# The two halves of each weight made by transfers instead of a cast and a subtraction, with ten buffers for each half

## The chip, the cores and the metric

The kernel runs on one core of a Trainium2 chip. The metric is the device time of one launch in microseconds (us), all inputs lying in device memory at its start. A smaller number is better. The time before is the median of three runs, 2927.23 us (2926.73 to 2929.2).

## The reference

A small transformer backbone: two layers over 512 latent tokens and 256 context tokens of width 1024. Each layer is a half-weighted SwiGLU feed-forward block, a token mixer, and another such block; each is modulated by vectors computed from a conditioning vector, and closed by a layer norm. Cut to what matters here, float32 throughout:

```python
def swiglu(u, w_in, w_out):
    a, v = jnp.split(u @ w_in, 2, axis=-1)
    return (jax.nn.silu(a) * v) @ w_out

def ffn_sublayer(h, shift, scale, gate, w_in, w_out, g, b):
    y = swiglu(modulate(h, shift, scale), w_in, w_out)     # h * (1 + scale) + shift
    return layer_norm(ALPHA * h + FFN_RES * gate * y, g, b)

for i in range(DEPTH):                                      # 2
    h_lat, h_ctx = ffn_sublayer(...), ffn_sublayer(...)     # first block
    y = neighborhood_attention(...) if i == 0 else window_gqa(...)
    h_lat = layer_norm(ALPHA * h_lat + m_lat[5] * y_lat, ...)
    h_lat = ffn_sublayer(...)                               # second block (and h_ctx in layer 0)
return h_lat
```

Mixer 0 is a two-dimensional neighbourhood attention with a learned relative bias; mixer 1 is a windowed attention with rotary positions. All weights together are some 158 blocks of 1 MB.

## The kernel before

**The arithmetic.** TensorE multiplies a rounded kind of float32, here called F32R. To keep float32 accuracy every factor is held as two F32R tiles: the hi part, its rounded value, and the lo part, what is left of it. A product is three matmuls (`mm3`, lines 114 to 116): hi by hi, lo activation by hi weight, hi activation by lo weight. The names are `uh`/`ul` for the modulated input, `gh`/`gl` for the gated middle of a feed-forward block, `wh`/`wl` for the weights, `z` for the residual stream, `pa`, `pv`, `pd`, `pq`, `pk` for tiles of PSUM.

**The weights.** The host lays them out in the order of use as units of 128 x 2048. `wunit` (lines 86 to 103) fetches a unit as four tiles of 128 x 512 float32, 256 KB each. For each tile SP issues a load into a raw tile `wr` (three buffers), ACT copies it with rounding to `wh` (line 99), and POOL subtracts the two into `wl` (line 100). `wh` and `wl` have nine buffers each, handed out in turn, so a tile's copy waits until TensorE has read the tile nine back. The last unit of each feed-forward block takes its tiles from another pool instead (`slabs`), and a few units are fetched a second time (`again`, tiles with a b at the end of their names).

**The stages.** A feed-forward block (`ffn`) runs over 11 chunks of 256 middle columns; each chunk uses three units, two for the up projections and one for the down projection. The tokens are taken in two groups, 512 latent and 256 context tokens; the last block (1b) has only the latent ones, in two groups of 256. So 1b spends fewer matmuls on each unit than the other blocks. The mixers (`na_mixer`, `wa_mixer`) project queries, keys and values with such units; in the softmax POOL scales the rows (line 565, `scale_p`), and in mixer 1 POOL also makes one product of the rotary positions (line 763). At the start, four steps (`gemv`) multiply a modulation weight `wm` (1 MB pieces issued by SP) with the conditioning vectors, and the first matmuls with weights go in between. Two more modulation pieces (`wm` 4 and 5) follow in `late_gate`. `bias_tables` (lines 580 to 584) builds the relative bias of mixer 0 in device memory with 8 transfers into `xd` and 16 into `yd`, all issued by SP. Its first part is tied behind the latest weight load (`behind(..., loaded[0])`, a tie that holds only between instructions of the same engine). In the background DVE computes the other modulation vectors from `wt` tiles that SP loads.

**The order.** A scheduler simulates the program and sets the order of each engine's queue; each engine then runs its queue in that order. A DMA is issued by an engine's queue (SP, ACT or POOL) once what it waits for has come; a wait at the head of a queue holds all that stands behind it.

Of the kernel before, what the change touches and what calls it, by code (L numbers as in the profile page):

```python
# [8 lines left out]
F32 = mybir.dt.float32  # L9
F32R = mybir.dt.float32r  # L10
BF16 = mybir.dt.bfloat16
I32 = mybir.dt.int32
AF = mybir.ActivationFunctionType
ALU = mybir.AluOpType
# [4 lines left out]
P = 128  # L19
# [17 lines left out]
def hybrid_kernel(ctx: ExitStack, tc: tile.TileContext, h0, cc, crow, wmod, wmodt, bmod, lnp, wst,  # L37
                  rpbp, nmask, sinks, ropec, rmat, ident, wmask, out):
    nc = tc.nc
    cp = ctx.enter_context(tc.tile_pool(name="cp", bufs=1))  # L40
    rp = ctx.enter_context(tc.tile_pool(name="rp", bufs=1))
    wp = ctx.enter_context(tc.tile_pool(name="wp", bufs=1))
# [41 lines left out]
    wpos, loaded = [0], [None]  # L84

    def wunit(slabs=False, again=None):
        i = wpos[0] if again is None else again
        if again is None:
            wpos[0] += 1
        hs, ls = [], []  # L90
        for q in range(4):
            nm = f"{i}_{q}" + ("" if again is None else "b")
            raw = wp.tile([P, 512], F32, tag="wr", name=f"wr{nm}", bufs=3)
            loaded[0] = nc.sync.dma_start(raw[:], wst[i, :, q * 512:(q + 1) * 512])
            if slabs:
                hi, lo = [sp.tile([P, 512], F32R, tag="slab", name=f"w{x}{nm}", bufs=SLABS) for x in "hl"]
            else:
                hi, lo = [wp.tile([P, 512], F32R, tag=f"w{x}", name=f"w{x}{nm}", bufs=9) for x in "hl"]
            nc.scalar.copy(hi[:], raw[:])  # L99
            nc.gpsimd.tensor_tensor(out=lo[:], in0=raw[:], in1=hi[:].bitcast(F32), op=ALU.subtract)  # L100
            hs.append(hi)
            ls.append(lo)
        return hs, ls
# [295 lines left out]
    def ffn(nm, groups, gt, mid, post, units=(), opened={}, head=None, apart=None):  # L399
# [4 lines left out]
        def unit(slabs=False):  # L404
            return units.pop(0) if units else wunit(slabs)
# [32 lines left out]
        for ci in list(range(NCH)) + [("r", NCH - 2)]:  # L438
# [3 lines left out]
            if late:  # L442
                again = i0
            w = [wunit(again=again + i) if r else unit(ci == NCH - 1 and i == 2) for i in range(3)]
            cn = f"r{ci[1]}" if r else f"{ci}"
            gs = [[gp.tile([P, NT], F32R, tag="gs", name=f"g{x}{nm}_{cn}_{i}", bufs=6) for x in "hl"] for i in range(2)]
# [13 lines left out]
            if r:  # L460
                avs((b, 0), (b, 1))
                dn(b)
                post(1)
            elif late:
                avs((a, 0), (a, 1))
                dn(a)
            elif ci == NCH - 1:
                avs((a, 0), (a, 1))
                dn(a)
                avs((b, 0), (b, 1))  # L470
                post(0)
                dn(b)
            elif ci == 0 and apart:
                apart()
                avs((head[0], 0), (head[0], 1))
                dn(head[0])
                w[0:2] = [wunit(again=i0 + i) for i in range(2)]
                avs(*[(g, i) for g in head[1:] for i in range(2)])
                for g in head[1:]:
                    dn(g)  # L480
            else:
                avs(*([(g, i) for g in head for i in range(2)] if ci == 0 else [(a, 0), (b, 0), (a, 1), (b, 1)]))
                dn(a)
                dn(b)
# [624 lines left out]
```

## Time and profile before

| | us |
|---|---|
| median of 3 runs | 2927.23 |
| the profiled execution's own time | 2926.03 |
| its span, from the first to the last instruction | 2924.2 |
| TensorE (PE) busy | 2802.8 |
| DVE busy | 1842.5 |
| POOL busy | 1247.8 |
| ACT busy | 1033.0 |
| time of the packets of queue q1, as a share of 16 DMA engines | 32.1% |

The profile is of one execution. PE is the matmul side of TensorE, PEld its weight loads. A group's row names line, engine, operation, output and inputs, count, then busy time and the mean of one in ns, then the idle time of the engine before them with what ended it. A row of waits names who waited, for whom, the total, the number of times and the longest. In a view by time, a row is a start, a duration and the instructions merged in it; a bracket holds the idle time before. "SPq" marks what SP's queue issues.

### The profile page before, as it was taken

How to read it: one execution, taken by the hardware profiler on the slowest of the kernel's cores; microseconds unless marked ns; L12 is line 12 of the kernel's file. 1: busy time of each engine (PE TensorE's matmuls, PEld its weight loads, DVE VectorE, ACT ScalarE, POOL GpSimd, SP SyncE). 2: the span in 40 equal slices, each digit the busy share in tenths (PEclk: the TensorE clock that was granted, in tenths of full speed). 3: DMA queues.
4: the chain of work that ended last, by engine and by line, in shares of the span. 5: the costliest groups of instructions: out<-in, count | busy, mean ns of one | idle time of the engine just before them, and what ended most of it. 6: DMA issues, size and time to landing. Idle time of an engine off the chain costs nothing. (4 is left out here: it accounts for less than half of the span.)

```text
span 2924.2 us, 49325 instructions
## 1 busy us (share of the span) xinstructions
PE 2802.8 (96%) x18106; PEld 2470.4 (84%) x18106; DVE 1842.5 (63%) x5023; ACT 1033.0 (35%) x2122; POOL 1247.8 (43%) x1102
## 2 busy tenths in 40 slices
PE   8899999989999979999999899999998999899997
PEld 5788888888888869888888788888887777799997
DVE  3489994375545685767675757776358667733335
ACT  4122122266455452222223522121236655533333
POOL 4233232465433563332335623232456544644453
PEclk9999999999999989999999999999999999899998
DMA  7444442232211312343432324342321111233332
GB/s 290 147 148 145 134 138 61 85 89 80 66 50 52 108 60 87 109 126 109 122 96 87 112 87 121 108 125 73 87 85 55 51 37 30 76 94 96 97 108 81
DMA packets 165842, 286.05 MB, mean 98 GB/s; under 512 B 25952, under 2 KB 38368, under 8 KB 164576
## 3 DMA queue, kind: packets, MB, share of 16 engines
q1 hardware_dynamic: 165312, 282.76, 32.1%
q8 instruction: 142, 2.33, 0.3%
q14 instruction: 100, 0.82, 0.1%
q10 hardware_dynamic: 288, 0.14, 0.0%
HBM read 280.74 MB, written 6.48 MB: 98 GB/s over the span
## 5 line engine op out<-in xcount | busy, mean ns | idle before, releaser
L100 POOL TENSOR_TENSOR wl<-wr,wh 128x512 fp32r<-128x512 f32 x632 | 834.4, 1333 | 1226.7 <-ACT wh L99 1002.3
L99 ACT CAST wh<-wr 128x512 fp32r<-128x512 f32 x632 | 388.9, 620 | 738.4 <-DMA wr<-in_wst_dram 324.4
L172 DVE CUSTOM_DVE_ANT_0 jk<-wt,cb 128x256 f32<-128x256 f32 x960 | 489.3, 544 | 0.0
L395 DVE SCALAR_TENSOR_TENSOR z<-pd1a,gt,z 128x512 f32<-128x512 f32 (+1 forms) x168 | 103.0, 619 | 89.8 <-PE pd1a L116 89.6
L395 DVE SCALAR_TENSOR_TENSOR z<-pd0a,gt,z 128x512 f32<-128x512 f32 (+1 forms) x168 | 102.9, 618 | 83.9 <-PE pd0a L116 83.4
L395 DVE SCALAR_TENSOR_TENSOR z<-pd0b,gt,z 128x256 f32<-128x256 f32 (+1 forms) x176 | 105.0, 600 | 76.6 <-PE pd0b L116 76.5
L114 PE MATMUL pa0a<-uh,wh 128*128 128x512 f32 (+1 forms) x328 | 113.8, 347 | 14.8 <-ACT wh L99 10.9
L114 PE MATMUL pd0a<-gh0a,wh 128*128 128x512 f32 (+1 forms) x336 | 114.9, 345 | 2.9 <-DVE z L395 2.9
L114 PE MATMUL pd0b<-gh0b,wh 128*128 128x256 f32 (+1 forms) x352 | 116.7, 334 | 0.3 <-DVE z L395 0.3
L115 PE MATMUL pd0b<-gl0b,wh 128*128 128x256 f32 (+1 forms) x352 | 116.7, 332 | 0.0
L116 PE MATMUL pd0b<-gh0b,wl 128*128 128x256 f32 (+1 forms) x352 | 116.6, 332 | 0.0
L114 PE MATMUL pa1a<-uh,wh 128*128 128x512 f32 (+1 forms) x336 | 114.7, 341 | 1.2 <-DVE uh L259 1.2
L114 PE MATMUL pd1a<-gh1a,wh 128*128 128x512 f32 (+1 forms) x336 | 113.7, 342 | 1.3 <-DVE z L395 0.7
L114 PE MATMUL pv1a<-uh,wh 128*128 128x512 f32 (+1 forms) x336 | 114.6, 341 | 0.0
L115 PE MATMUL pv1a<-ul,wh 128*128 128x512 f32 (+1 forms) x336 | 114.5, 341 | 0.0
L115 PE MATMUL pa1a<-ul,wh 128*128 128x512 f32 (+1 forms) x336 | 114.3, 340 | 0.0
L116 PE MATMUL pd0a<-gh0a,wl 128*128 128x512 f32 (+1 forms) x336 | 114.3, 341 | 0.0
L115 PE MATMUL pd0a<-gl0a,wh 128*128 128x512 f32 (+1 forms) x336 | 114.3, 340 | 0.0
L116 PE MATMUL pv1a<-uh,wl 128*128 128x512 f32 (+1 forms) x336 | 114.2, 340 | 0.0
L115 PE MATMUL pd1a<-gl1a,wh 128*128 128x512 f32 (+1 forms) x336 | 114.2, 340 | 0.0
L116 PE MATMUL pa1a<-uh,wl 128*128 128x512 f32 (+1 forms) x336 | 114.2, 340 | 0.0
L116 PE MATMUL pd1a<-gh1a,wl 128*128 128x512 f32 (+1 forms) x336 | 114.0, 340 | 0.0
(882 smaller groups left out, 9238.2 us busy)
## 6 DMA issues: line engine op xcount, KB each, us to landing
wr<-in_wst_dram SPq DMA_DIRECT2D x632, 256.0 KB
wt<-in_wmodt_dram SPq DMA_DIRECT2D x240, 256.0 KB
wm<-in_wmod_dram SPq DMA_DIRECT2D x8, 1024.0 KB
nb<-yd SPq DMA_DIRECT2D x60, 128.0 KB
wr_0b<-in_wst_dram SPq DMA_DIRECT2D x19, 256.0 KB
wr_1b<-in_wst_dram SPq DMA_DIRECT2D x19, 256.0 KB
wr_2b<-in_wst_dram SPq DMA_DIRECT2D x19, 256.0 KB
wr_3b<-in_wst_dram SPq DMA_DIRECT2D x19, 256.0 KB
```

The lines of the kernel that those rows point to most:

```text
L99: nc.scalar.copy(hi[:], raw[:])
L100: nc.gpsimd.tensor_tensor(out=lo[:], in0=raw[:], in1=hi[:].bitcast(F32), op=ALU.subtract)
L114: nc.tensor.matmul(ps, a[0], b[0], start=first, stop=False)
L115: nc.tensor.matmul(ps, a[0], b[1], start=False, stop=False)
L116: nc.tensor.matmul(ps, a[1], b[0], start=False, stop=last)
L172: x = nc.vector.tensor_tensor_reduce(out=junk[:, 0:256], in0=w[:, q * 256:q * 256 + 256], in1=cb[2 * st + half][:, q * 256:q * 256 + 256], ...
L395: last[0] = nc.vector.scalar_tensor_tensor(out=zt(d, c0, c1), in0=pd, scalar=gt[:, d, st:st + 1], in1=zt(d, c0, c1), op0=ALU.mult, op1=ALU ...
```

## The change

The raw tile goes. The hi part is loaded from device memory straight into the F32R tile, by a transfer that rounds, issued by POOL. ACT writes the negated hi part into the lo tile. A second transfer, also issued by POOL, reads the same float32 weights again and adds them to the lo tile, which then holds weight minus hi. The subtraction on POOL and the load on SP are gone; the weights are read twice. The hi and lo rings have ten buffers instead of nine.

```diff
         for q in range(4):
             nm = f"{i}_{q}" + ("" if again is None else "b")
-            raw = wp.tile([P, 512], F32, tag="wr", name=f"wr{nm}", bufs=3)
-            loaded[0] = nc.sync.dma_start(raw[:], wst[i, :, q * 512:(q + 1) * 512])
             if slabs:
                 hi, lo = [sp.tile([P, 512], F32R, tag="slab", name=f"w{x}{nm}", bufs=SLABS) for x in "hl"]
             else:
-                hi, lo = [wp.tile([P, 512], F32R, tag=f"w{x}", name=f"w{x}{nm}", bufs=9) for x in "hl"]
-            nc.scalar.copy(hi[:], raw[:])
-            nc.gpsimd.tensor_tensor(out=lo[:], in0=raw[:], in1=hi[:].bitcast(F32), op=ALU.subtract)
+                hi, lo = [wp.tile([P, 512], F32R, tag=f"w{x}", name=f"w{x}{nm}", bufs=10) for x in "hl"]
+            loaded[0] = nc.gpsimd.dma_start(hi[:], wst[i, :, q * 512:(q + 1) * 512])
+            nc.scalar.activation(lo[:], hi[:].bitcast(F32), AF.Copy, scale=-1.0)
+            nc.gpsimd.dma_start(lo[:], wst[i, :, q * 512:(q + 1) * 512], accum_op=ALU.add)
             hs.append(hi)
             ls.append(lo)
```

From here on the changed kernel's line numbers are one less than those of the kernel before; line 97 is the rounding load, 98 the negated copy, 99 the adding transfer. Since the latest weight load is now issued by POOL, the tie of the bias tables behind it no longer binds.

SP's queue around the bias tables (`xd`, `yd`), before, in the first feed-forward block; `wr` are weight tiles, `wt` tiles of the background modulation:

```order
L94 DMA wr_2_876<-in_wst_dram 128x512
L94 DMA wr_3_882<-in_wst_dram 128x512
L582 DMA xd<-in_rpbp_dram 16x63x8 x8
L168 DMA wt_28_0_1301<-in_wmodt_dram 128x512
L168 DMA wt_28_1_1327<-in_wmodt_dram 128x512
L168 DMA wt_29_0_1349<-in_wmodt_dram 128x512
L584 DMA yd<-xd 128x1x504 x16
L94 DMA wr_0_1455<-in_wst_dram 128x512
L94 DMA wr_1_1461<-in_wst_dram 128x512
```

The same queue now, in the part from the last input tile (`z`) to the end of the late modulation pieces (`wm`):

```order
L917 DMA z_98<-in_h_dram 128x768
L576 DMA nsink<-in_sinks_dram 128x16
L581 DMA xd<-in_rpbp_dram 16x63x8 x8
L148 DMA wm_4_0_507<-in_wmod_dram 128x512
...
L148 DMA wm_5_3_547<-in_wmod_dram 128x512
L583 DMA yd<-xd 128x1x504 x16
L148 DMA wm_5_4_549<-in_wmod_dram 128x512
L148 DMA wm_5_5_551<-in_wmod_dram 128x512
```

The tables have moved from behind the weights of the second chunk to the start, and no weight tile stands behind them any more.

POOL's queue in a chunk of the last feed-forward block, before; each row is the subtraction of one tile:

```order
L100 TENSOR_TENSOR wl_2_28444<-wr_2_28441,wh_2_28443 128x512
L100 TENSOR_TENSOR wl_3_28450<-wr_3_28447,wh_3_28449 128x512
L100 TENSOR_TENSOR wl_0_28456<-wr_0_28453,wh_0_28455 128x512
L100 TENSOR_TENSOR wl_1_28462<-wr_1_28459,wh_1_28461 128x512
L100 TENSOR_TENSOR wl_2_28468<-wr_2_28465,wh_2_28467 128x512
```

The same place now:

```order
L97 DMA wh_2_28251<-in_wst_dram 128x512
L97 DMA wh_3_28256<-in_wst_dram 128x512
L97 DMA wh_0_28261<-in_wst_dram 128x512
L97 DMA wh_1_28266<-in_wst_dram 128x512
L99 DMA wl_2_28252<-in_wst_dram 128x512
L99 DMA wl_3_28257<-in_wst_dram 128x512
L99 DMA wl_0_28262<-in_wst_dram 128x512
L99 DMA wl_1_28267<-in_wst_dram 128x512
L97 DMA wh_2_28271<-in_wst_dram 128x512
L97 DMA wh_3_28276<-in_wst_dram 128x512
L99 DMA wl_2_28272<-in_wst_dram 128x512
```

Each subtraction has become two issues, often four hi loads and then their four adding transfers.

POOL's queue in mixer 1, where the queries of the next heads are projected, before; `qeq` is the rotary product, `pw` a scaling of the softmax:

```order
L763 TENSOR_TENSOR qeq_0_25402<-qeq_0_25402,rc_23556 128x512
L100 TENSOR_TENSOR wl_1_26044<-wr_1_26041,wh_1_26043 128x512
L100 TENSOR_TENSOR wl_2_26050<-wr_2_26047,wh_2_26049 128x512
L100 TENSOR_TENSOR wl_3_26056<-wr_3_26053,wh_3_26055 128x512
L100 TENSOR_TENSOR wl_0_26140<-wr_0_26137,wh_0_26139 128x512
L763 TENSOR_TENSOR qeq_1_25441<-qeq_1_25441,rc_23556 128x512
L565 TENSOR_SCALAR pw_0_0_25565<-pw_0_0_25565,l_0_25547 128x512
```

The same place now:

```order
L762 TENSOR_TENSOR qeq_0_24862<-qeq_0_24862,rc_23044 128x512
L97 DMA wh_2_25501<-in_wst_dram 128x512
L97 DMA wh_3_25506<-in_wst_dram 128x512
L97 DMA wh_0_25589<-in_wst_dram 128x512
L99 DMA wl_2_25502<-in_wst_dram 128x512
L97 DMA wh_1_25594<-in_wst_dram 128x512
L99 DMA wl_3_25507<-in_wst_dram 128x512
L99 DMA wl_0_25590<-in_wst_dram 128x512
L762 TENSOR_TENSOR qeq_1_24901<-qeq_1_24901,rc_23044 128x512
L564 TENSOR_SCALAR pw_0_0_25021<-pw_0_0_25021,l_0_25003 128x512
```

Between the two rotary products stand seven issues, three of them adding, in place of four subtractions.

## The prediction

> **What bounds the kernel now.** I read the page's busy times first, then busy time by stage, then what TensorE waits for. On the page, the first line gives busy time and share of the span for each engine:
>
> ```profile
> PE 2802.8 (96%) x18106; PEld 2470.4 (84%) x18106; DVE 1842.5 (63%) x5023; ACT 1033.0 (35%) x2122; POOL 1247.8 (43%) x1102
> ```
>
> TensorE is busy in all but 121 us of 2924. The change takes no matmul away, so it can win only from those 121 us, and can lose wherever a weight comes late. The waits of TensorE, longest in total first (total, times, longest single one):
>
> ```profile
> PE prl L323 <- DVE yl L293: 19.6, 8, 5.8
> PE pvl L367 <- DVE aql L283: 12.1, 3, 5.5
> PE pa0a L114 <- ACT wh L99: 10.9, 1, 10.9
> ```
>
> The first two are layer norms, untouched. The third is the one large wait for a weight, and it is one event. The view by time shows where (SPq and ACT rows, then TensorE's):
>
> ```profile
> 118.22 15.27 SPq L584 DMA_DIRECT2D yd<-xd  x16
> 134.27 3.03 SPq L94 DMA_DIRECT2D wr<-in_wst_dram  x3
> 144.46 1.93 ACT L99 CAST wh<-wr 128x512 fp32r<-128x512 f32 x3 [17.71 <-DMA wr<-in_wst_dram]
> 145.12 0.79 PE L114 MATMUL pa0a<-uh,wh 128*128 128x512 f32 x1 [10.94 <-ACT wh L99]
> 149.13 0.62 PE L114 MATMUL pd0a<-gh0a,wh 128*128 128x512 f32 x1
> 149.56 0.43 PE L115 MATMUL pd0a<-gl0a,wh 128*128 128x512 f32 x1
> 150.53 0.39 PE L115 MATMUL pa0a<-ul,wh 128*128 128x512 f32 x1
> 150.76 0.39 PE L116 MATMUL pa0a<-uh,wl 128*128 128x512 f32 x1
> ```
>
> The sixteen bias-table transfers sit on SP ahead of three weight loads, so those are issued at 134 and land at 144. The last four rows show TensorE's pace: starts 0.43 us apart at 149, 0.23 at 150.5.
>
> The stages, us from the start (busy and count of PE, PEld, DVE, ACT, POOL; granted clock; DMA share; GB/s). They are: start, rest of FFN 0a, mixer 0, FFN 0b, its end, FFN 1a, mixer 1, FFN 1b, end:
>
> ```profile
> 0.00:150.00 150.00, 126.58 (x674) 94.44 (x675) 57.40 (x154) 47.35 (x82) 47.70 (x47) 0.95 0.64 217
> 150.00:575.00 425.00, 422.40 (x2363) 368.11 (x2363) 316.02 (x1057) 96.00 (x173) 144.59 (x108) 1.00 0.40 119
> 575.00:1100.00 525.00, 490.68 (x3614) 435.67 (x3613) 343.43 (x866) 276.91 (x614) 275.62 (x281) 0.97 0.25 73
> 1100.00:1550.00 450.00, 450.00 (x2612) 396.90 (x2612) 315.17 (x988) 105.23 (x187) 153.66 (x116) 1.00 0.37 109
> 1550.00:1680.00 130.00, 122.50 (x712) 107.83 (x711) 81.00 (x150) 55.81 (x102) 74.33 (x61) 0.97 0.31 94
> 1680.00:2200.00 520.00, 516.56 (x2965) 454.06 (x2963) 321.40 (x898) 129.84 (x228) 187.31 (x144) 1.00 0.33 99
> 2200.00:2540.00 340.00, 305.54 (x2114) 247.56 (x2115) 252.39 (x591) 196.55 (x494) 185.84 (x206) 0.95 0.15 44
> 2540.00:2850.00 310.00, 309.40 (x2618) 308.98 (x2618) 117.31 (x223) 99.10 (x190) 150.42 (x118) 1.00 0.34 100
> ```
>
> **The subtraction goes, two POOL issues come.** The groups of costliest instructions, and the same view by stage for line 100 alone (POOL busy and count):
>
> ```profile
> L100 POOL TENSOR_TENSOR wl<-wr,wh 128x512 fp32r<-128x512 f32 x632 | 834.4, 1333 | 1226.7 <-ACT wh L99 1002.3
> 575.00:1100.00 525.00, 133.06 (x101) 0.97 0.25 73
> 1550.00:1680.00 130.00, 47.99 (x35) 0.97 0.31 94
> 2200.00:2540.00 340.00, 77.86 (x57) 0.95 0.15 44
> 2540.00:2850.00 310.00, 149.49 (x117) 1.00 0.34 100
> ```
>
> With the 4 x 19 second loads there are 708 tiles: 708 subtractions go, 1416 transfers are issued on POOL. No transfer is issued there today, so its price c is unknown. SP's issues bound it (min/median/max in ns):
>
> ```profile
> L94 SPq DMA_DIRECT2D wr<-in_wst_dram x632: 327/328/1213, 3.3 to 2853.4; - x158
> L641 SPq DMA_DIRECT2D nb<-yd x60: 514/592/2099, 659.8 to 1005.8; - x60
> ```
>
> So c lies between 0.33 and 2.10 us. I take 1.33, the row of the POOL instruction on the same tile that it replaces. The load by stage is POOL's other work plus 2c per tile. FFN 1b: 150.42 - 149.49 + 234c, which at 1.33 is 312 us of the stage's 310. End of 0b: 26.3 + 70c = 119 of 130. Mixer 1: 108 + 114c = 260 of 340. Mixer 0: 142.6 + 202c = 411 of 525. FFN 0a, 0b and 1a have 214, 230 and 272 issues in 425, 450 and 520 us, under 75%: free. FFN 1b is the stage that decides; it keeps up below c = 1.32.
>
> POOL runs in order, and the new issues wait in its queue. A hi load waits until TensorE has read the tile ten back, which today SP and ACT wait for. An adding transfer waits for ACT's negated copy, and so for the hi part to land. What POOL waits for in 1b today:
>
> ```profile
> POOL wl L100 <- ACT wh L99: 102.7, 46, 8.2
> POOL wl L100 <- PE pv1b L115: 40.8, 11, 5.5
> POOL wl L100 <- PE pv1b L116: 12.8, 7, 2.0
> ```
>
> The 53.6 us behind TensorE remain, now with issues and with the adding transfers of the tiles that TensorE needs next queued behind them. How far ahead the ring is: four of ten tiles are in use, and six at 310/117 = 2.65 us are 16 us. How long a tile of a batch of four takes: four issues, a landing of 3.5 us (below), 0.6 on ACT, one issue more and a second landing, 5 x 1.33 + 7.6 = 14.3 us. That just fits, with no room for a wait. If all 53.6 us add to a full queue, 1b grows by 2 + 54 = 56 us; if the ring absorbs them, by 2. I take half the wait: **+29 us** (ends: 0 at c = 0.33, and +182 at 2.10, from 234 x 2.10 + 0.9 - 310, without waits).
>
> In mixer 1 the second rotary product (L763), which the scores wait for, stands behind four subtractions:
>
> ```profile
> 2375.02 1.29 POOL L763 TENSOR_TENSOR qeq<-qeq,rc 128x512 f32<-128x512 f32 x1 [11.02 <-PE prq L760]
> 2379.09 4.14 POOL L100 TENSOR_TENSOR wl<-wr,wh 128x512 fp32r<-128x512 f32 x3 [0.89 <-PE wq L116]
> 2383.64 1.29 POOL L763 TENSOR_TENSOR qeq<-qeq,rc 128x512 f32<-128x512 f32 x1 [0.41 <-PE prq L760]
> ```
>
> It then stands behind seven issues, three of them adding. From the end of the first product to the second is 7.3 us now; 7 x 1.33 + 3.5 for a landing + 0.6 on ACT is 13.4. So it comes 6 us later, in three such places; TensorE has other matmuls for half: **+9 us**. In mixer 0, 101 tiles add 101 x (2.66 - 1.32) = 135 us of POOL work, among the scalings of the softmax:
>
> ```profile
> L565 POOL TENSOR_SCALAR p<-p,l 128x512 f32<-128x512 f32 x64 | 44.8, 700 | 105.0 <-DVE l L663 87.8 <-DVE m L660 7.0 <-PE oc L558 6.9
> L565 POOL TENSOR_SCALAR p_c<-p_c,l_c 128x256 f32<-128x256 f32 x32 | 15.0, 484 | 25.6 <-DVE l_c L689 25.4
> ```
>
> POOL is idle 131 us before those today, so most of it is hidden. I take a tenth, **+13 us**. End of 0b, at 92%: **+3 us**. Ends for these three: 0, and at c = 2.10 mixer 0 has 567 us of work in 525, mixer 1 347 in 340, the end of 0b 173 in 130, +92 together.
>
> The 3.5 us for a landing is from two rows, SP's issue and the ACT copy that waited:
>
> ```profile
> 146.46 0.33 SPq L94 DMA_DIRECT2D wr<-in_wst_dram  x1
> 149.98 0.62 ACT L99 CAST wh<-wr 128x512 fp32r<-128x512 f32 x1 [3.60 <-DMA wr<-in_wst_dram]
> ```
>
> **The stall at 134.** Weights leave SP, so the tables no longer stand ahead of them: -10.9 us. After the stall TensorE runs at half pace, from 145.12 to 149.56 in the rows above; the granted clock of the stretch shows it:
>
> ```profile
> 125.00:150.00 25.00, 14.06 (x57) 11.23 (x56) 10.51 (x43) 2.28 (x5) 3.75 (x3) 0.80 0.59 201
> ```
>
> Half of those 4.4 us, 2.2, goes too: **-13 us** (ends -13 and 0). The tables move ahead of the last four pieces of a modulation weight; the 15.27 us of issue there may delay a gate. Before, SP issued weight loads in that time, so I take 0 (to +15).
>
> **The start.** Today three weight tiles are issued before the second modulation piece; then ten go out on POOL at once:
>
> ```profile
> 0.00:25.00 25.00, 14.55 (x54) 7.17 (x55) 6.67 (x13) 8.05 (x12) 6.96 (x11) 1.00 0.93 369
> ```
>
> At 369 GB/s and 93% busy, seven tiles of 262 KB more take 5 us from the pieces that TensorE waits for: **+5 us** (0 to +7). The eight adding transfers by 50 us fit into idle DMA time.
>
> **ACT** gets one instruction of the same shape for each of these:
>
> ```profile
> L99 ACT CAST wh<-wr 128x512 fp32r<-128x512 f32 x632 | 388.9, 620 | 738.4 <-DMA wr<-in_wst_dram 324.4
> ```
>
> It keeps its 620 ns: nothing, while its input lands in time; if a landing is late, the gating products of the FFN stand behind it on ACT. The raw tiles' room gives one more buffer per half, which loses the three tiles read ahead: counted in the waits above.
>
> **Sum** for the profiled execution (2926.03 us): -13 + 5 + 29 + 9 + 13 + 3 = +46, so 2972; the median of the runs is 1.2 higher: **2973 us**.
>
> **Rivals.** *Cheap issues.* At c of 1.0 or less, FFN 1b has 235 of 310 us of POOL work and 12.6 of its 16 us for a batch, so the ring absorbs the waits, and the stall is gone: 2927 - 13 + 5 = 2919, or up to 2932 where the new order costs the mixers a little. For it: SP's 0.33. Against it: POOL's scaling of half a tile is 0.48 in the row above, and its queue now also waits for landings. The Trainium skill, DMA: Bandwidth & Descriptors, Latency and other measured facts, puts the first byte at about 1 us for transfers issued from GpSimd and 0.6 from SP; 0.4 more than SP's issue is 0.73, an estimate, and the sum by it is this rival's 2919. No run here shows it.
>
> *The adding transfers are slow* (the slower side). An adding one reads its target too. In 1b 0.34 x 310 = 105 us of all DMA engines carry 117 plain tiles, 0.9 us each. At twice the price for the adding ones the sum is 316 us, full; at three times 421: +111, and FFN 0a, 0b and 1a pass their lengths by 34, 27 and 19: 2927 - 8 + 191 = 3110. It decides from twice on. At c = 2.10 POOL gives as much: +182 in 1b, +92 above, +120 in the other FFNs, 3313. Against: the shares of 0.15 to 0.40 leave room.
>
> *The stall stays*, because the tables and the weights share the DMA engines and not only SP: 13 us more, 2932 at cheap issues. The Trainium skill, DMA: Bandwidth & Descriptors, Issuing engines are not separate DMA queues, says just that several issuers save only sequencer time. The trace goes against its "small": 15.27 us are SP's time.
>
> **Chances.** Forecast (2935 to 3060) 0.38; cheap issues 0.34, of which 0.24 under 2921; slow adding or issues over 1.8 us (3060 to 3320) 0.22; stall stays, at cheap issues, 0.06. A measurement tells 0.2%, 5.9 us, from no change. Faster is the 0.24; same is 0.10 of cheap issues and the 0.06; slower is the rest, 0.60. The range 2906 to 3190 leaves out 0.04 below and 0.12 above; the forecast's own is 2935 to 3060.
>
> **What would show it.** POOL's issue rows give c: 1.33 confirms the sum, under 1.0 the first rival. FFN 1b over 330 us with POOL over 90% and TensorE waiting for wl by DMA is the forecast; the same with POOL under 80% and DMA over 0.9 is the second. TensorE without a wait over 5 us between 100 and 160 shows the stall gone. The forecast is wrong if 1b keeps its 310 us.

## The result, and the profile after

The changed kernel takes 3085.05 us (median of four runs, 3074.91 to 3086.74), the kernel before 2928.13 us beside it: a ratio of 1.0529, with a 95% interval of 1.0505 to 1.0553. The forecast was 2973. The profiled execution has a span of 3073.1 us, 148.9 more than before. The lines of the page that answer to those quoted of before, busy time first, then the DMA queues:

```profile
PE 2859.6 (93%) x18106; PEld 2502.8 (81%) x18106; DVE 1576.1 (51%) x5023; ACT 1016.5 (33%) x2122; POOL 1316.3 (43%) x1810
...
q0 software_dynamic: 203904, 371.29, 58.7%
q1 hardware_dynamic: 63360, 97.12, 9.7%
```

TensorE is without work for 213 us where it was for 121, and its own busy time is 57 us longer, at a mean granted clock of 0.967 for 0.983; 23 of these 57 are in the last FFN (377 us for 354, at 0.96 for 0.99). POOL is busy for the same share as before. What TensorE waits for now, the two largest rows (total, times, longest):

```profile
PE gm L131 <- DMA wm<-in_wmod_dram: 34.3, 8, 13.2
PE pa1b L115 <- DMA wl<-in_wst_dram: 26.9, 31, 2.5
```

They are the modulation weights at the start, 7.4 us before, and low parts in the last FFN; together 61 of the 213 us, and the rest is in many small waits. The last FFN's gate matmuls before and after (view of the tile `pa1b`: least/median/longest ns, first and last start):

```profile
L116 PE MATMUL pa1b<-uh,wl x320: 274/283/415, 2513.9 to 2870.6; 128*128 128x256 f32 x160
```

```profile
L115 PE MATMUL pa1b<-uh,wl x320: 274/283/583, 2606.6 to 3017.8; 128*128 128x256 f32 x160
```

Read in the same way for the other stages (first start to last start of a stage's first matmul group, us), the difference is spread; what the rows leave out is 3 us:

| stretch | before | after | difference |
|---|---|---|---|
| start, to the last gemv matmul | 74.5 | 111.0 | +36.5 |
| from there to FFN 0a's last gate matmul | 510.5 | 504.3 | -6.2 |
| to FFN 0b's first (mixer 0) | 474.7 | 489.9 | +15.2 |
| FFN 0b, first to last | 539.0 | 557.8 | +18.8 |
| FFN 1a, first to last | 537.1 | 548.4 | +11.3 |
| FFN 1a's last to FFN 1b's first (mixer 1) | 346.4 | 362.1 | +15.7 |
| FFN 1b, first to last | 358.0 | 412.6 | +54.6 |

The last row is what is called "the stretch" below. The busy time by stage for it:

```profile
2605.00:3017.00 412.00, 376.56 (x2953) 366.29 (x2954) 125.70 (x295) 121.88 (x241) 200.36 (x281) 0.96 0.80 166
```

POOL works 200 of 412 us and the DMA engines are at 0.80: neither is full. What the new operations cost (rows by line over the whole run, then the landings of each line's transfers in the stretch, high parts and then low parts; a landing is counted from the start of the issue):

```profile
L99 POOL DMA_DIRECT2D wl<-in_wst_dram x632 | 595.2, 1079 | 698.4 <-ACT wl L98 437.2
L98 ACT ACTIVATE wl<-wh 128x512 fp32r<-128x512 f32 x632 | 392.3, 630 | 1105.6 <-DMA wh<-in_wst_dram 984.4
L97 POOL DMA_DIRECT2D wh<-in_wst_dram x632 | 430.2, 805 | 634.0 <-PE pd0b L115 125.3
```

```profile
DMA to landing us min/median/max: 3.2/6.2/9.2
...
DMA to landing us min/median/max: 4.1/6.0/9.2
```

The middle row is the one to look at: ACT waits 984 us in all for high parts to land, and POOL then 437 us for ACT. A tile's way is a chain: place free, issue, landing, copy, issue, landing. Such totals show where the chain waits, not what it costs: the kernel with two rounding transfers, below, has 769 and 426 at 2951 us.

### The profile page after: what moved, and what is told of

Read it like the earlier page. It is cut to its first block, busy times and chain, and to the rows that moved or that the text cites. A ratio compares the mean times of both kernels' runs of the same rounds, so it can differ in the third digit from the quotient of the medians.

```text
span 3073.1 us, 49526 instructions
## 1 busy us (share of the span) xinstructions
PE 2859.6 (93%) x18106; PEld 2502.8 (81%) x18106; DVE 1576.1 (51%) x5023; ACT 1016.5 (33%) x2122; POOL 1316.3 (43%) x1810
## 3 DMA queue, kind: packets, MB, share of 16 engines
q0 software_dynamic: 203904, 371.29, 58.7%
## 4 chain that ended last, share of the span: by engine, by line
issue 32%; PE 28%; POOL 17%; DMA 14%; DVE 5%; ACT 3%; SPq 0%; POOLq 0%; ACTq 0%; DVEq 0%
DMA wh<-in_wst_dram 9%; POOL wl L99 8%; POOL wh L97 5%; DMA wl<-in_wst_dram 2%; PE wo L557 1%; ACT wl L98 1%; PE o L557 1%; PE tp L548 1%; PE pa1b L115 1%; PE vn L113 1%; DMA z<-in_h_dram 1%; PE vn L115 1%; PE vn L114 1%; DVE aql L282 1%; PE pq L113 1%
## 5 line engine op out<-in xcount | busy, mean ns | idle before, releaser
L99 POOL DMA_DIRECT2D wl<-in_wst_dram x632 | 595.2, 1079 | 698.4 <-ACT wl L98 437.2
L98 ACT ACTIVATE wl<-wh 128x512 fp32r<-128x512 f32 x632 | 392.3, 630 | 1105.6 <-DMA wh<-in_wst_dram 984.4
L97 POOL DMA_DIRECT2D wh<-in_wst_dram x632 | 430.2, 805 | 634.0 <-PE pd0b L115 125.3
L171 DVE CUSTOM_DVE_ANT_0 jk<-wt,cb 128x256 f32<-128x256 f32 x960 | 366.7, 420 | 0.0
L394 DVE SCALAR_TENSOR_TENSOR z<-pd1b,gt,z 128x256 f32<-128x256 f32 x147 | 70.3, 483 | 107.2 <-PE pd1b L115 106.0
L115 PE MATMUL pa1b<-uh,wl 128*128 128x256 f32 x320 | 96.2, 301 | 27.0 <-DMA wl<-in_wst_dram 26.9
L115 PE MATMUL pa0a<-uh,wl 128*128 128x512 f32 (+1 forms) x328 | 112.9, 344 | 6.3 <-DMA wl<-in_wst_dram 6.3
```

The costliest lines, as they stand in the source:

```text
L97: loaded[0] = nc.gpsimd.dma_start(hi[:], wst[i, :, q * 512:(q + 1) * 512])
L98: nc.scalar.activation(lo[:], hi[:].bitcast(F32), AF.Copy, scale=-1.0)
L99: nc.gpsimd.dma_start(lo[:], wst[i, :, q * 512:(q + 1) * 512], accum_op=ALU.add)
L115: nc.tensor.matmul(ps, a[1], b[0], start=False, stop=last)
L171: x = nc.vector.tensor_tensor_reduce(out=junk[:, 0:256], in0=w[:, q * 256:q * 256 + 256], in1=cb[2 * st + half][:, q * 256:q * 256 + 256], ...
L394: last[0] = nc.vector.scalar_tensor_tensor(out=zt(d, c0, c1), in0=pd, scalar=gt[:, d, st:st + 1], in1=zt(d, c0, c1), op0=ALU.mult, op1=ALU ...
```

## The experiments

Eighteen kernels ran. "Tables" are the bias tables, "the stretch" is the last FFN's from above, and "engine work" is a queue's share times the span: for instance 58.7% of 3073.1 us over 708 tiles is 2.55 us of all sixteen engines per tile. Where no range is given, a kernel ran once; the four runs of the changed kernel itself lie within 12 us.

### The start: tables behind the modulation weights

The SP rows of the changed kernel from 38 us on (start, duration, line, transfers):

```profile
38.12 18.72 SPq L581 DMA_DIRECT2D xd<-in_rpbp_dram  x8
56.94 8.76 SPq L148 DMA_DIRECT2D wm<-in_wmod_dram  x12
66.14 20.32 SPq L583 DMA_DIRECT2D yd<-xd  x16
87.33 9.11 SPq L148 DMA_DIRECT2D wm<-in_wmod_dram  x4
```

The transfers of xd stand ahead of all sixteen modulation pieces and those of yd ahead of the last four, since the weight load that held them back is on POOL now. The edit ties them to the last piece instead (`wm_end` is set where the pieces are issued, which is not shown):

```diff
-behind(nc.sync.dma_start(xd[:, r], ...), loaded[0])
+behind(nc.sync.dma_start(xd[:, r], ...), wm_end[0])   # the last modulation piece
```

> The changed kernel with one edit: the bias tables are held behind the last piece of the two modulation weights on SP's queue. Theory START: the 39 us that SP spends on issuing the tables (18.72 for xd, 20.32 for yd) ahead of and among those pieces put the last gemv matmul at 111 us where it was at 74.5; with the edit it comes before 90 us and the run is 25 to 40 us shorter than the changed kernel's 3085, so 3045 to 3060. Rival: the eight engines' worth of early transfers fill the DMA engines (share 1.08 from 25 to 50 us), the order on SP only decides who waits; the last gemv matmul stays after 100 us and the time within 10 us of 3085.

Measured: 3082.9 us; the last gemv matmul came at 86.4 us where it was at 111.0. So 24.6 of the 36.5 us at the start are the tables, and half of the expectation held; the other 11.9 were not tried. FFN 0a ended 11 us earlier than in the changed kernel, and of that 2 us were left at the end of FFN 1a. The second half failed: the time did not move. The same edit where the low part comes by a rounding transfer (the kernel of the next part):

> The kernel with two rounding transfers per tile (output not the reference's) and the bias tables behind the last piece of the modulation weights. START: where the FFNs have room, the 25 us that the last gemv matmul gains (111 to 86 with the adding) are kept: last gemv matmul before 85 us, FFN 0a's last gate matmul at 570 to 578 where it was 591.8, run 2925 to 2940. Rival: the gain is lost again within FFN 0a, as half of it was with the adding; the run stays within 6 of 2951.

Measured: 2944.1 us, the last gemv matmul at 84.5, FFN 0a's last gate matmul at 582.6. That is between the two: 9 us are kept at FFN 0a's end, and 7 at the end of the run. The start is thus not worth what it loses there: later work that waits for weights takes most of it back.

### The adding transfer against a second rounding one

```diff
-nc.gpsimd.dma_start(lo[:], wst[...], accum_op=ALU.add)
+nc.gpsimd.dma_start(lo[:], wst[...])
```

> The changed kernel with a second rounding transfer in the place of the adding one: the low part is then the rounded weight itself and the output is not the reference's; issues, waits and order stay. ENGINES: if the adding is what is dear, the software queue's share falls from 58.7% by at least a quarter, the last FFN's stretch falls from 412 us to under 380 and the run to under 3050. LATENCY: the two landings stay in series; the stretch stays at 395 us or more, the run over 3060.

Measured: 2951.13 us, with POOL's order unchanged. The software queue, and the landings in the stretch:

```profile
q0 software_dynamic: 203904, 371.29, 46.9%
```

```profile
DMA to landing us min/median/max: 3.2/4.2/6.7
...
DMA to landing us min/median/max: 3.4/4.0/6.3
```

46.9% of 2949.4 us over 1416 transfers is 0.98 us for a rounding transfer, so an adding one takes 2.55 - 0.98 = 1.57; a plain one took 0.905 before (32.1% of 2924.2, less 9.7% of 3073.1 for what is not weights, over 708). The adding is what is dear in this order, as ENGINES said, and the stretch fell to 364 us; only the queue's share fell by a fifth and not by a quarter. But the landings fell too, by 2 us each, so this run alone does not tell work from time.

Half of each adding transfer:

> The changed kernel whose adding transfer covers only the left 256 of 512 columns (the right half of each low part stays the negated high part, so the output is not the reference's). WORK (the adding transfer's use of the engines, 1.57 us of all sixteen for 512 columns, sets the loss): 0.98 + 0.79 = 1.77 us per tile is under the 1.95 of two rounding ones, so the last FFN's stretch is 366 us or less and the run 2960 or less. FIXED (each adding transfer has a longer landing and issue of its own, whatever its size): the stretch stays over 395 and the run over 3040. If both go with the size, the run lies between.

Measured: 2967.18 us, the stretch 368. An adding issue still took 0.89 us at half the size, and POOL was busy 44%, 43% in the changed kernel. The issue's price is therefore not what costs; landings of the low parts in the stretch were 3.8 us (median). FIXED failed, and WORK's bounds were missed by 2 us in the stretch and by 7 in the run, in an order that is new.

### Engine work, time and POOL's work put back one by one

On the kernel with two rounding transfers, three extras: a spare transfer per tile for the engines, a second ACT pass for time, a memset for POOL (`x` is the low part's issue).

```diff
+nc.sync.dma_start(spill[(4 * i + q) % 8], hi[:, 0:336].bitcast(F32))           # spill
+nc.scalar.activation(lo[:], lo[:].bitcast(F32), AF.Copy, scale=1.0)            # late
+behind(nc.gpsimd.memset(fill[:], 0.0), x)                                      # issue
```

> The kernel with two rounding transfers per tile (so the low part is again not the reference's), and behind each high part that has landed a plain transfer from SP's queue that writes 336 of its 512 columns to a scratch area that nobody reads: by 0.905 us for a whole plain tile about 0.59 us of all engines, what an adding transfer took more than a rounding one. ENGINES: the engines' work per tile is back at 2.55 us, so the last FFN's stretch goes back from 364 us to 395 or more and the run from 2951 to over 3040. LATENCY (what costs is the adding transfer's own time: least landing 4.1 us for 3.2, issue 0.89 for 0.53): the stretch stays under 375 and the run under 2990.

> The kernel with two rounding transfers per tile (output not the reference's) and a second pass of ACT over each negated copy: 0.63 us more between a high part's landing and the low part's issue, no more engine work, no more POOL work. TIME (what the adding costs is the longer way of each tile: 0.9 us of landing, 0.36 us of issue): half of that way is back, so the run goes from 2951 to 2985 or more. WORK: under 2965.

> The kernel with two rounding transfers per tile (output not the reference's) and on POOL, behind each low part's issue, a memset of 128x256 to a tile that nobody reads, some 0.3 us, about what an adding issue takes more than a rounding one (0.89 for 0.53). TIME by way of POOL: the issues behind it come later, the run is 2970 or more. If POOL has room (36% busy): under 2960.

> The kernel with two rounding transfers per tile (output not the reference's) and all three extras together: the spare transfers of 336 columns, the second ACT pass, the memset on POOL. SUM (they add as they did one by one, 31 + 13 + 9 over 2951): 2995 to 3015. COUPLED (each takes the room that hid the others): 3035 or more, towards the changed kernel's 3085.

Measured: 2981.93 with the spare transfers (0.50 us of engine work each, 2.45 per tile; stretch 389), 2964.51 with the second pass (369), 2960.42 with the memset (0.33 us; 367). Of the expectations for one extra, WORK held for the second pass, by half a microsecond; with spare transfers LATENCY held for the run and not for the stretch; the memset run fell between its two bounds. The three together gave 2972.89 (stretch 382), less than the spare transfers alone. So both SUM and COUPLED failed: the adding's extras, one by one or together, do not rebuild its 124 us (from a span of 2949.4 to one of 3073.1). The scheduler wrote new orders for these kernels, and some 10 us of such sums may be the order's. The same spare transfers on the changed kernel itself:

> The changed kernel with the same spare transfers of 336 columns: landings and issues of the weights keep their own price, the engines' work per tile rises from 2.55 to about 3.1 us. ENGINES: the last FFN's stretch rises from 412 us to over 445, the run to over 3200. LATENCY: it stays under 425, the run under 3130.

Measured: 3170.7 us, the stretch 440 at an engine share of 0.90, both between the bounds of the two theories. The engines had room that the changed kernel, at 0.80, did not use; yet the run got longer. The landings in the stretch rose to 6.7 and 7.1 us.

### What goes with the stretch: the two landings

The kernels above, all with ten places, by the two median landings in the stretch (the two with moved tables lie within 2 us of their pairs):

| kernel | high + low landing, us | stretch, us |
|---|---|---|
| two rounding | 4.2 + 4.0 = 8.2 | 364 |
| with memset | 4.3 + 4.0 = 8.3 | 367 |
| with second pass | 4.6 + 3.7 = 8.3 | 369 |
| half adding | 4.7 + 3.8 = 8.5 | 368 |
| all three extras | 5.1 + 4.7 = 9.8 | 382 |
| with spare transfers | 5.1 + 5.5 = 10.6 | 389 |
| changed kernel | 6.2 + 6.0 = 12.2 | 413 |
| changed, with spare transfers | 6.7 + 7.1 = 13.8 | 440 |

The stretch follows the sum of landings. But the engines' work per tile puts these kernels in nearly the same order (1.88 to 1.96 us in the first four, 2.46 and 2.45 in the two with spare transfers after them, 2.55 and 3.04 in the last two), so the table alone does not tell landings from work.

The prediction gave a tile 16 us from its place's release to its use. Paired in their order, the rows of lines 97 to 99 in the stretch give 13.3 us (median of 118 tiles) from the start of the high part's issue to the landing of its low part in the changed kernel, and 9.5 with two rounding transfers. The issues of a batch of four start some 0.66 and 0.53 us apart, so a batch's last tile is ready about 15.3 and 11.1 us after the first could be issued. The first leaves 0.7 us for any wait, the second 4.9. The next runs put that to the test by changing the places.

### The ring's places

```diff
-hi, lo = [wp.tile(..., bufs=10) for x in "hl"]
+hi, lo = [wp.tile(..., bufs=9) for x in "hl"]                          # nine and nine
+hi, lo = [wp.tile(..., bufs=11 if x == "h" else 10) for x in "hl"]     # eleven and ten
+hi, lo = [wp.tile(..., bufs=10 if x == "h" else 11) for x in "hl"]     # ten and eleven
+hi, lo = [wp.tile(..., bufs=12 if x == "h" else 9) for x in "hl"]      # twelve and nine
```

> The changed kernel with nine tiles per ring where it has ten. Theory LATENCY: a tile holds its place in the ring for two landings in series, a copy, two issues and its use, about 10 x 3.52 = 35 us in the last FFN (412 us from its first to its last gate matmul, 117 tiles); with nine places a tile takes 35.2/9 = 3.9 us, so that stretch grows by about 45 us and the run is 3140 or more. Rival ENGINES: the DMA engines' own work on rounding and adding transfers sets the pace (1.27 us of all sixteen for each); the ring's length then matters little, the stretch stays within 8 us of 412 and the run within 15 of 3085.

Measured: 3133.26 us, 48 more, but the stretch grew by 15 us and not by 45; the rest is in the other three FFNs (+12 to +15 each). LATENCY's direction held; its size was missed, by 7 us in the run (3140 or more) and by 30 in the stretch. ENGINES failed.

> The changed kernel with eleven high tiles to ten low ones (the room left by the raw tiles). LATENCY: one tile more in flight gives back some of the 48 us that one less took: 3055 to 3075. If the low tiles' ring or the engines bind instead: within 8 of 3085.

Measured: 3005.96 us (3003.36 to 3010.97), a ratio to before of 1.0266 (1.0247 to 1.0285): 79 us back from one place, where 30 was the most expected; its stretch is 390 us, in a new order.

> The changed kernel with the one spare place given to the low parts: ten high, eleven low; every engine's order is that of the changed kernel. TWO LANDINGS: a low place is wanted only when the high part has landed, so a spare one shortens nothing: within 10 us of 3085. Rival (any place more helps, as the eleventh high one did): 3040 or less.

Measured: 3078.43 us (3076.61 to 3083.44), ratio 1.0516 (1.0495 to 1.0536), the changed kernel's within its scatter. A place more for the low part is worth nothing, with every engine's queue in the changed kernel's order. Its stretch is 409 us, and TensorE waits there as it did:

```profile
PE pa1b L115 <- DMA wl<-in_wst_dram: 28.4, 27, 2.8
```

> The changed kernel with twelve high and nine low places, 21 as in the run with eleven and ten (3006). TWO LANDINGS: the high part of a tile is fetched two tiles further ahead than its low part's place, so less of the first landing lies behind the release: 2975 to 3000. Rival (the sum of places or the shorter ring counts, as with nine and nine): 3010 or more.

Measured: 2976.92 us (2974.36 to 2980.61), ratio 1.0164 (1.0147 to 1.0181). With the same 21 places as eleven and ten, and one low place fewer than the changed kernel, 108 us are back. Its stretch, in the view by stage:

```profile
2551.00:2918.00 367.00, 357.11 (x2924) 351.69 (x2924) 126.77 (x297) 127.80 (x249) 201.98 (x282) 0.99 0.89 186
```

TensorE's wait for low parts there, which was 26.9 us, and ACT's wait for high parts in the whole run, which was 984.4:

```profile
PE pa1b L115 <- DMA wl<-in_wst_dram: 2.4, 4, 0.9
...
ACT wl L98 <- DMA wh<-in_wst_dram: 310.7, 156, 7.1
```

The adding transfers are all there, engine work is 2.50 us per tile (59.4% of 2976.7 over 708), and the landings are even longer (6.2 and 7.2 us), but more of the first now lies ahead of the low place's release: the negated copy begins 1.2 us after the high part has landed (median in the stretch, 2.7 in the mean), where it began within 0.1 us in the changed kernel. The stretch is 367 us with the engines at 0.89. So in the last FFN neither the engines' work nor the landings as such set the changed kernel's time, but two landings in a row behind one release. What remains open: the orders of the two kernels with more high places are new ones too; only the ten-and-eleven run and the one with two rounding transfers have the changed kernel's very order. And 49 us over the kernel before remain: 39 are lost at the start, of which the rest of FFN 0a makes up 21, 12 in FFN 0b, 12 in the mixers and 9 in the last FFN.

### The negated copy on DVE

```diff
-nc.scalar.activation(lo[:], hi[:].bitcast(F32), AF.Copy, scale=-1.0)
+nc.vector.tensor_scalar(out=lo[:], in0=hi[:].bitcast(F32), scalar1=-1.0, scalar2=None, op0=ALU.mult)
```

> The changed kernel with the negated copy on DVE where it is on ACT. LATENCY: the copies no longer stand behind the gating products on ACT (POOL waited 35 us for sl and gh in the last FFN); that stretch gets 10 to 30 us shorter than 412, the run 3030 to 3075. ENGINES: no change there, within 8 us of 412.

Measured: 3064.31 us, 21 fewer, but only 4 of them in the stretch (409). The run is as LATENCY said, the place is not: the copies' standing behind the gating products was not what cost in the last FFN. Its order is a new one.

### One part of the change alone

The kernel before, with only the adding (raw tiles stay) and with only the rounding (raw tiles and subtraction stay):

```diff
-nc.gpsimd.tensor_tensor(out=lo[:], in0=raw[:], in1=hi[:].bitcast(F32), op=ALU.subtract)
+nc.scalar.activation(lo[:], hi[:].bitcast(F32), AF.Copy, scale=-1.0)
+nc.gpsimd.dma_start(lo[:], wst[...], accum_op=ALU.add)                # adding alone
...
-nc.scalar.copy(hi[:], raw[:])
+nc.gpsimd.dma_start(hi[:], wst[...])                                  # rounding alone
```

> The kernel before with one part of the change: raw tiles on SP and the rounding copy on ACT stay, POOL's subtraction becomes ACT's negated copy and POOL's adding transfer. ENGINES: 0.905 + 1.57 us of all engines per tile are nearly the changed kernel's 2.55, so the run is 3030 or more. Rival (the high part's rounding transfer, queued on POOL among the adding ones, is what makes tiles late): the high parts come early again; under 2985. ACT has 392 us more, 74 of them in the last FFN.

> As the run with the kernel before and adding transfers (3009), but the raw tiles are loaded from POOL's queue too, by plain transfers: nothing is rounded by a transfer, and loads and adding transfers share one queue and one engine's order as in the changed kernel. SHARED QUEUE: a load stands behind adding transfers that wait for ACT, so the run goes to 3050 or more. Rival (the queue does not matter, the engines' work does): within 20 of 3009.

> The kernel before with the other part of the change alone: the high part by a rounding transfer on POOL, the raw tile still on SP and the low part still POOL's subtraction, so each weight is read twice (0.98 + 0.9 us of all engines per tile) and nothing is added. If adding is the whole loss: 2925 to 2955. If reading twice and POOL's queue cost by themselves: 2975 or more.

Measured: adding alone 3008.84 us (stretch 396); with its raw tiles loaded from POOL's queue 2962.43 (stretch 368); rounding alone 3025.84 (stretch 381). The first lies between its two bounds, the second below both: POOL's queue does no harm here, as the run with everything on it is 46 us faster than the one with raw tiles on SP, and at the same engine work (56.9% of 2960.6 is 2.38 us per tile with its adding; 36.1% of 3007.1 for the adding and 0.85 for the raw tile are 2.38). In both, a raw tile is fetched ahead of the place, so only one landing follows the release. That fits the second; it does not explain the first, whose stretch is 396 us, with 18.7 us of TensorE's waits for low parts there for 3.7. The third is the rival's: reading twice with no adding costs 97 us in this form. There POOL's subtraction waits for a landing, with the next high loads' issues queued behind it:

```profile
POOL wl L100 <- DMA wh<-in_wst_dram: 278.2, 177, 4.3
POOL wl L100 <- DMA wr<-in_wst_dram: 123.5, 74, 25.4
```

Why SP's raw tiles cost 46 us more than POOL's is open; the two have different orders, and their low parts land alike (7.0 and 6.7 us).

### The tables alone, on the kernel before

```diff
 def bias_tables():          # called in chunk 1: the eight transfers of xd
+def bias_rows(h0):          # called in chunks 2 to 9: two transfers of yd, behind a weight load
```

> The kernel before with the sixteen table transfers of yd issued two at a time behind the weights of the FFN's third to tenth chunk, so that no three weight loads stand behind 15 us of issue. If the stall at 134 us and the half pace after it are SP's time, as the prediction says: 13 us less, 2912 to 2920. If the stall comes back in another place or at the start: 2925 to 2935.

Measured: 2914.81 us (2913.12 to 2917.12), ratio 0.9957 with an interval of 0.9943 to 0.9970. TensorE's busy time from 100 to 150 us, where the stall was:

```profile
100.00:150.00 50.00, 50.00 (x295) 44.14 (x294) 35.05 (x118) 11.65 (x21) 16.72 (x13) 1.00 0.47 116
```

This is the fastest kernel of the study, 0.4% under the kernel before.

## Why the prediction was off

The sum was +46 and the profiled run grew by 148.9. By stage, the missing 103 us are 32 at the start, 7 in the rest of FFN 0a, 30 in FFN 0b and 1a together, 26 in FFN 1b and 9 in the mixers.

**The stall at 134: right, and of the right size.** It is gone after the change (no wait of TensorE over 5 us between 103 and 160 us), and the run with spread tables is 13.4 us faster than before, for -13.

**POOL's issue price: the term that the sum was built on, and wrong.** The prediction took c = 1.33 from the subtraction. A rounding issue took 0.53 us (median of the run with two of them), an adding one 0.89. Beside adding ones the row of a rounding issue is 0.86 too, but there the rows overlap, and four in a batch take 2.8. So POOL was never full: 200 of 412 us in the last FFN, where 312 of 310 were forecast. The Trainium skill's sentence on first bytes (DMA: Bandwidth & Descriptors, Latency and other measured facts), about 1 us from GpSimd for 0.6 from SP, had given the estimate of 0.73, which lies between these two rows. But the rival worked out from it, 2919, went wrong with the rest, because the price of an issue was not what decided.

**FFN 1b: +29 forecast, +54.6 measured. The step that failed is "a landing of 3.5 us" in the sum of 14.3 that "just fits", and with it the half of the waits that the ring was to absorb.** It had the right chain and took for both landings a plain transfer's 3.5 us from a row at 0.59 engine share. They took 6.2 and 6.0 in that stage. Two other errors went the other way: the issues were cheaper than 1.33, and since the 3.5 us already run from the issue's start, two of the five issues were counted twice. So the measured way is still under 16 us, at 15.3. What failed is that such a chain has no room: of the 53.6 us of waits the prediction let the ring absorb half, and the stage lost about as much as all of them, though POOL was far from full. With landings of 4.2 and 4.0 us in the same order the stage lost 5.8 us.

The prediction wrote that the three tiles read ahead are "counted in the waits above". The waits there are POOL's of before, measured with these tiles in place. Giving their room to low places is worth nothing, as ten and eleven shows, where two more high places and one low place fewer bring 108 us in the run and all but 9 us of the stage's loss. How 15.3 of 16 us become 54.6 is not worked out by any run.

The same Trainium skill page (Anatomy of one DMA, SWDGE path) fits a transfer from GpSimd at 2.0 us and 1 us per 436 KB, which for 262 KB is an estimate of 2.6; the least landings here, counted from the start of the issue, were 3.2 (rounding) and 4.1 us (adding), and the medians under load those above, so the measurement decides.

**"FFN 0a, 0b and 1a free": wrong.** FFN 0b lost 18.8 and FFN 1a 11.3 us. They were called free because POOL has room there, but the loss follows the landings and the places: with two rounding transfers in the same order they lost 4.6 and 1.2 us, and nine and nine places took another 12 to 15 us from each. By the prediction's six tiles they have more time than FFN 1b (520 us for 136 tiles in FFN 1a, 23 us for six), so the sum above does not give their loss; which wait does stays open.

**The start: +5 forecast, +36.5 there.** The term held the tables to be ahead of the last four modulation pieces only and took 0 (to +15) for that; xd stood ahead of all sixteen, as the order of SP's queue shows that is printed ahead of the prediction, and 24.6 us were the tables. The reason given, that SP issued weight loads in that time before, fails on the row: the two groups of table issues take 39 us on SP, and the weight loads before took 0.33 us each. How much of the 36.5 reaches the end is small: putting the tables back gave 0 with adding transfers and 7 without.

**The mixers: +22 forecast, about +31 measured** (15.2 and 15.7). The direction held; by which wait was not tried.

**The rival of slow adding transfers** had its price nearly right: 1.57 us are 1.74 times a plain transfer, just under the twice from which it was to decide. Its mechanism, full engines, was not what happened: the stage ran at 0.80, and at 0.89 it took 367 us with twelve high places. The sign that was to tell the two apart (POOL over 90%, or the engines over 0.9) fitted neither: POOL 49%, engines 0.80. A stage in which nothing is full and everything waits is a chain. The prediction wrote this chain down, but had no case in which it decides.

## What to carry to other kernels

When a change gives up read-ahead buffers, write out what stands between the release of a place and the use of the next tile in it, with landings taken at the load that the change will bring and not from today's row; if two landings come one behind the other, try the room on the tile that is fetched first. And when a transfer moves to another queue, look for what was ordered by it: here tables that were held behind a weight load came loose.

## What the hardware showed beside that

POOL's subtractions slowed DVE. The background products on DVE, two tiles read from SBUF, before and after (busy, mean ns):

```profile
L172 DVE CUSTOM_DVE_ANT_0 jk<-wt,cb 128x256 f32<-128x256 f32 x960 | 489.3, 544 | 0.0
```

```profile
L171 DVE CUSTOM_DVE_ANT_0 jk<-wt,cb 128x256 f32<-128x256 f32 x960 | 366.7, 420 | 0.0
```

They take 541 ns again in the kernel with rounding alone, which keeps the subtractions, and 418 in the one with adding alone, which has none. The Trainium skill (GPSIMD Engine Reference, Specifications) names this contention for DVE instructions with two SBUF inputs, and the trace agrees. It brought DVE 123 us; what it brought the run was not tried.

An adding transfer of half a tile still used 0.90 us of the engines (44.8% of 2965.4 over 708, less 0.98), for 1.57 of a whole one: 57% for half the size.
